# Three hand-overs of an encoder: weight operands in idle token tiles, Newton steps behind the sums, rates one product later

## Chip, core and metric

The kernel runs on one core of one Trainium2 chip. The metric is the device time of one execution in microseconds (us): the median of three runs. The core's engines have queues of their own: PE (TensorE, matrix products), DVE (VectorE, elementwise), ACT (ScalarE, elementwise), SP (which issues the DMAs).

## What is computed

An encoder of two residual layers over one sequence of 512 tokens with 1024 channels, in float32. Layer 0 mixes tokens by a Fourier transform, layer 1 by retention with four heads; each is followed by a SwiGLU channel mixer. Every sub-layer begins with an RMS norm, whose result is scaled and shifted by vectors that come from a conditioning vector c; one norm stands at the end.

```
for i in range(DEPTH):                       # DEPTH = 2
    mod = c_act @ w_ada[i] + b_ada[i]
    sh1, sc1, g1, sh2, sc2, g2 = jnp.split(mod, 6, axis=-1)
    h = modulate(rmsnorm(x, norm_mix_g[i]), sh1, sc1)
    m = fourier_mixer(h, w_o) if i % 2 == 0 else retention_mixer(h, w_in, w_out, ...)
    x = x + g1 * m
    h = modulate(rmsnorm(x, norm_ffn_g[i]), sh2, sc2)
    x = x + g2 * swiglu(h, w_ffn_in[i], w_ffn_out[i])
return modulate(rmsnorm(x, final_norm_g), shf, scf)
```

## The kernel before

**Operands.** x is held transposed, channels on the 128 partitions, in four tiles `x0` to `x3`. A float32 product is made of three passes with rounded operands: every operand is split into a high part (a cast on ACT, L201 in `split`) and a low part (source minus high, on DVE, L202), and PE adds high by high, high by low and low by high. Weights arrive by DMA in `raw` tiles of 128x1024 (eight buffers, loaded up to four ahead by `issue`), and `high_low` splits each into a tile of the pool `high` and one of the pool `low`, five buffers each.

**Units.** The wide products (kinds "v", "qk", "g" of retention, "fi" of the channel mixer) are done by `Unit`, 512 tokens by 512 columns at a time, with seven quarter-size products in place of eight. Each product has a tag ("1", "2", "7", "6", "5", "3", "4") and is 24 matmuls of 128x256 on PE (L874). Its weight operand is a quarter or a sum of quarters; the sums are made on DVE by `combined` (L333). Its token operand is one of seven that `Quarters` makes from the modulated x, each a high and a low tile that is held for the whole stage (`a0` to `a6` the highs, `a7` to `a13` the lows). Tags "1" and "2" need only the first 256 tokens (t = 0), the other five also need the last 256 (t = 1). A finished quarter of the result is taken out of PSUM by an ACT copy (L883) and a DVE addition (L887).

**A turn.** A stage ends in `out_product_last`: the output product of the half of tokens t = 0 and then of t = 1, each piece added to x on DVE (L546, `add_gated`). Behind the additions the norm of the next stage runs: `sums` transposes squares-to-be on PE (L418), squares and sums them on ACT (L424), and scales the sums on DVE (L426, L428); `rate` runs three Newton steps on two columns on DVE (`rsqrt_steps`, L218, L226, L229) and turns the two columns into a row on PE (two transposes, L439); `half` modulates x (L462 on DVE, L466 and L467 on ACT) and makes the token operands (L493, L512, L202). For t = 0 this is done inside the output product. For t = 1 it is done by `first_units`, while the first products of the next stage (tags "1" and "2" of the first three units u0, u1, u2) run on PE. There are three such turns: into the channel mixer of layer 0 (`channels=True`, about 100 to 152 us of the trace; called A here), into retention (465 to 547 us; B) and into the channel mixer of layer 1 (893 to 938 us; C). The last turn, into the final norm, has no Units behind it.

**What sets the order.** The order of work comes from the list `program` that `first_units` and its like fill, from the step list that makes weight operands ahead of their use (`use_next`), and from a scheduler that places each instruction in its engine's queue; the norm's work stands under `tc.high_priority`. An engine takes its queue strictly in order. In turn B the retention's queries and keys are rotated by DVE operations at L1015 to L1018 before the first scores (L207 to L209 with `t4k` operands).

Of the kernel before, what the change touches and what calls it, by code (L numbers as in the profile page):

```python
# [11 lines left out]
F32R = mybir.dt.float32r  # L12
# [4 lines left out]
P = 128  # L17
D = 1024
# [18 lines left out]
URGENT = 500  # L37
# [116 lines left out]
def trunk(ctx, tc, A, where, out):  # L154
# [7 lines left out]
    highs = pool("high", 5)  # L162
    lows = pool("low", 5)
# [7 lines left out]
    def ps():  # L171
        return psum.tile([P, 512], F32, name="ps")
# [7 lines left out]
    def held(tag, dtype=F32R):  # L180

        return hpool.tile([P, D], dtype, name=tag)

    def tok(m):
        return slice(m * P, (m + 1) * P)
# [10 lines left out]
    def k4(t):  # L196
        return t.rearrange("p (k c) -> p k c", k=4)

    def split(dst_h, dst_l, src):

        nc.scalar.copy(out=dst_h, in_=src)  # L201
        nc.vector.tensor_tensor(out=dst_l, in0=src, in1=f32(dst_h), op=ALU.subtract)  # L202
# [33 lines left out]
    def rsqrt_of(columns):  # L236
        ys = []
        for _ in rsqrt_steps(columns, ys):
            pass
        return ys  # L240
# [31 lines left out]
    def add(fn, *needs):  # L272
        program.append((needs, fn))

    steps, at, fresh = [], {}, []
    state = {"step": 0, "load": 0, "piece": 0}
    loads, ready, mods, opening, wide = {}, {}, {}, set(), set()
    closing, shares = [], {(0, 1): 2, (0, 0): 2, (0, 3): 4, (0, 4): 4}

    def pieces_of(step):  # L280
# [23 lines left out]
            loads[name] = t  # L304
            state["load"] += 1

    def high_low(raw):
        h = highs.tile([P, D], F32R, name="high")
        low = lows.tile([P, D], F32R, name="low")
        split(h, low, raw)  # L310
        return h, low

# [13 lines left out]
    def combined(step):  # L326


        kind, i, u, tag, _ = step
        r = lambda k, s: loads[kind, i, u, k, s]  # L330

        def minus(dst, p, q, eng=nc.vector):
            eng.tensor_tensor(out=dst, in0=p, in1=q, op=ALU.subtract)  # L333

        if tag == "1":
            o = high_low(r(0, 0))
        elif tag == "2":
            o = high_low(r(1, 0))
            if (kind, i, u) not in opening:
                minus(r(0, 0), r(0, 1), r(0, 0))  # L340
        elif tag == "7":
            if (kind, i, u) in opening:
                minus(r(0, 0), r(0, 1), r(0, 0))
                minus(r(0, 1), r(1, 1), r(0, 1))
            o = high_low(loads.pop((kind, i, u, 0, 1)))
        elif tag == "6":
            t2 = comb.tile([P, D], F32, name="t2")
            minus(t2, r(1, 1), r(0, 0))
            minus(r(1, 0), r(1, 0), t2)
            o = high_low(t2)  # L350
            if (kind, i, u) not in opening:
                minus(r(0, 1), r(1, 1), r(0, 1))
        else:
            o = high_low(loads.pop((kind, i, u, *{"5": (0, 0), "3": (1, 1), "4": (1, 0)}[tag])))
        return k4(o[0]), k4(o[1])
# [48 lines left out]
    class Norm:  # L404


        def __init__(self, i, sc, sh):
            self.key = (i, sc), (i, sh)
            self.turned, self.mean, self.r = {}, {}, {}
            self.start()  # L410

        def sums(self, t, j):

            for c in range(2):
# [15 lines left out]
                        )  # L430
                self.mean[t, c] = ss

        def rate(self, t):
            o = ps()
            self.r[t] = o[:, 0:256]
            with tc.high_priority(offset=URGENT):
                rs = rsqrt_of([self.mean[t, c] for c in range(2)])
            for c, r in enumerate(rs):
                nc.tensor.transpose(o[:, tok(c)], r.broadcast_to([P, P]), ident)  # L439

        def spread(self, t, k):
            for key in self.key:
                settle(key, 4 * k + 3)
            with tc.high_priority(offset=URGENT):
                for _ in self.half(t, k):
                    pass
# [162 lines left out]
    def last_sums():  # L609
        for j in range(ND - SUMS, ND):  # L610
            made["norm"].sums(1, j)

    made = {}

# [278 lines left out]
    def first_units(u0, u1, u2, channels=False):  # L893


        for u in (u0, u1, u2):
            opening.add(u.key)
        wide.add(u1.key)
        spread = lambda t, k: add(lambda: made["norm"].spread(t, k))
        if channels:  # L900
            add(last_sums)
            u0.p("1")
            u1.p("1")
            add(lambda: made["norm"].rate(1))
            spread(1, 0)
            u2.p("1")
            spread(0, 1)
            u0.ps("72")
            spread(1, 1)
            u1.p("2")  # L910
            u2.p("2")
        else:
            u0.p("1")
            add(last_sums)
            u0.p("2")
            u1.p("1")
            add(lambda: made["norm"].scale(1))
            u1.p("2")
            u2.ps("12")
            u0.p("7")  # L920
        for u, t in ((u0, "6"), (u1, "7"), (u0, "5"), (u1, "6"), (u0, "3"), (u0, "4"), (u1, "5")):
            u.p(t)
# [353 lines left out]
```

## Time and profile before

| | us |
|---|---|
| runs | 1263.14, 1263.08, 1271.62 |
| median | 1263.14 |
| profiled execution | 1267.04 |
| its span, first to last instruction | 1265.3 |
| PE busy | 1207.9 (95%) |
| DVE busy | 1066.0 (84%) |
| ACT busy | 585.2 (46%) |

A row of a timeline gives start, duration, engine, line, operation, output and inputs, how many were merged, and in brackets how long the engine stood idle ahead of it and for whom. Durations overlap: the distance between the starts of neighbours is what one costs. A row of waits gives who waited at which line for whose result, the total, the number and the longest, in us. A row of windows gives, for a stretch, the busy time of each engine with the number of instructions, the granted TensorE clock as a share of 2.4 GHz, the DMA's share and its rate.

### The profile page before, as it was taken

The numbers are of one execution on the slowest core, as the hardware profiler recorded it, in microseconds if no ns is written. First come the engines' busy times: TensorE is split into PE (matmuls) and PEld (weight loads), VectorE is DVE, ScalarE is ACT, GpSimd is POOL, SyncE is SP. The second block draws the span as 40 slices with busy tenths as digits, with TensorE's granted clock in tenths as the row PEclk, the third lists the DMA queues.
The fourth block names the chain that finished last, engine by engine and source line by source line (L and its number), as shares of the span: only waits on it lengthen the run. The fifth ranks groups of instructions, "written<-read, shape, count | busy, mean of one in ns | idle before, by whom it ended". The sixth has DMA issues, their size and how long they took to land.

```text
span 1265.3 us, 20931 instructions
## 1 busy us (share of the span) xinstructions
PE 1207.9 (95%) x8424; PEld 1134.1 (90%) x8424; DVE 1066.0 (84%) x1733; ACT 585.2 (46%) x885; POOL 0.9 (0%) x8
## 2 busy tenths in 40 slices
PE   6898799999999998889999999999899999999996
PEld 5787799899999998879999999988899899999986
DVE  7799999889799779989899899964899777878855
ACT  4615654343435436536365454521665334444523
POOL 0000000000000000000000000000000000000000
PEclk9999899999999999899999999999999999999999
DMA  9486068464644621314233245872024434344402
GB/s 369 171 297 243 17 186 286 138 223 135 217 133 154 213 101 66 103 64 141 91 101 115 84 151 183 309 238 100 18 70 155 158 115 155 117 150 133 134 1 67
DMA packets 59440, 186.64 MB, mean 148 GB/s; under 512 B 5968, under 2 KB 14544, under 8 KB 59344
## 3 DMA queue, kind: packets, MB, share of 16 engines
q1 hardware_dynamic: 59344, 185.31, 43.3%
q8 instruction: 66, 1.08, 0.4%
q14 instruction: 30, 0.25, 0.1%
HBM read 177.95 MB, written 7.34 MB: 146 GB/s over the span
## 4 chain that ended last, share of the span: by engine, by line
PE 85%; DVE 8%; ACT 4%; issue 1%; DMA 1%; SPq 0%; ACTq 0%
PE ps L874 48%; PE ps L207 12%; PE ps L209 11%; PE ps L208 11%; DVE low L202 2%; DVE a L202 1%; ACT t4k L467 1%; ACT high L201 1%; PE ps L418 1%; DVE t4k L493 1%; ACT a L466 1%; DVE raw L383 1%; DVE raw L333 1%; DMA t4k<-in_x 1%; PE ps L1094 1%
## 5 line engine op out<-in xcount | busy, mean ns | idle before, releaser
L201 ACT CAST high<-raw 128x1024 fp32r<-128x1024 f32 x266 | 277.7, 1051 | 298.7 <-PE ps L208 96.9
L874 PE MATMUL ps<-a,high 128*128 128x256 f32 x2912 | 392.2, 285 | 3.7 <-ACT a L512 2.8
L202 DVE TENSOR_TENSOR low<-raw,high 128x1024 fp32r<-128x1024 f32 x266 | 323.6, 1221 | 63.6 <-ACT high L201 61.5
L874 PEld LDWEIGHTS ps<-a,high 128*128 128x128 f32 x2912 | 370.9, 193 | 6.1 <-ACT a L512 3.0
L874 PE MATMUL ps<-a,low 128*128 128x256 f32 x1456 | 208.7, 287 | 8.0 <-DVE low L202 7.9
L874 PEld LDWEIGHTS ps<-a,low 128*128 128x128 f32 x1456 | 191.1, 195 | 8.9 <-DVE low L202 8.9
L207 PE MATMUL ps<-t4k,high 128*128 128x512 f32 (+1 forms) x512 | 182.2, 356 | 0.0
L208 PE MATMUL ps<-t4k,high 128*128 128x512 f32 (+1 forms) x512 | 179.0, 350 | 0.0
L209 PE MATMUL ps<-t4k,low 128*128 128x512 f32 (+1 forms) x512 | 178.7, 349 | 0.0
L383 DVE SCALAR_TENSOR_TENSOR raw<-raw,c_act 128x1024 f32<-128x1024 f32 x104 | 125.9, 1221 | 34.1 <-DMA raw<-in_w_ada 23.3
L874 PE MATMUL ps<-high,a 128*128 128x256 f32 x896 | 122.8, 284 | 4.6 <-ACT t2k L883 3.7
L874 PEld LDWEIGHTS ps<-high,a 128*128 128x128 f32 x896 | 114.8, 192 | 6.3 <-ACT t2k L883 4.1
L209 PEld LDWEIGHTS ps<-t4k,low 128*128 128x128 f32 x512 | 96.6, 189 | 12.7
L207 PEld LDWEIGHTS ps<-t4k,high 128*128 128x128 f32 x512 | 96.7, 189 | 11.9
L208 PEld LDWEIGHTS ps<-t4k,high 128*128 128x128 f32 x512 | 96.9, 189 | 11.6
L546 DVE SCALAR_TENSOR_TENSOR x<-ps,mod,x 128x512 f32<-128x512 f32 (+1 forms) x132 | 81.0, 634 | 29.7 <-PE ps L209 29.5
L883 ACT COPY t2k<-ps 128x512 f32<-128x512 f32 x102 | 59.6, 585 | 99.9 <-PE ps L874 96.8
L887 DVE TENSOR_TENSOR t2k<-t2k,ps 128x512 f32<-128x512 f32 x102 | 69.6, 683 | 12.4 <-ACT t2k L883 7.1
L333 DVE TENSOR_TENSOR raw<-raw 128x1024 f32<-128x1024 f32 x62 | 75.5, 1218 | 0.1
L874 PE MATMUL ps<-low,a 128*128 128x256 f32 x448 | 63.7, 285 | 0.0
L201 ACT CAST t4k<-t2k 128x512 fp32r<-128x512 f32 x76 | 46.8, 619 | 35.6 <-DVE t2k L939 20.0
L874 PEld LDWEIGHTS ps<-low,a 128*128 128x128 f32 x448 | 58.6, 194 | 0.0
(142 smaller groups left out, 1325.5 us busy)
## 6 DMA issues: line engine op xcount, KB each, us to landing
raw<-in_w_ada SPq DMA_DIRECT2D x88, 512.0 KB, 4.7
raw<-in_w_ffn_in SPq DMA_DIRECT2D x84, 512.0 KB, 4.2
raw<-in_w_ret_in SPq DMA_DIRECT2D x46, 512.0 KB, 3.3
raw<-in_w_ffn_out SPq DMA_DIRECT2D x44, 512.0 KB, 4.0
raw<-in_w_ret_out SPq DMA_DIRECT2D x16, 512.0 KB, 4.4
raw<-in_w_ada_final SPq DMA_DIRECT2D x16, 512.0 KB, 3.7
raw<-in_w_fourier_out SPq DMA_DIRECT2D x8, 512.0 KB, 6.9
z<-t2k SPq DMA_DIRECT2D x12, 256.0 KB, 3.1
```

Of the source, the lines that this page charges most:

```text
L201: nc.scalar.copy(out=dst_h, in_=src)
L202: nc.vector.tensor_tensor(out=dst_l, in0=src, in1=f32(dst_h), op=ALU.subtract)
L207: nc.tensor.matmul(o, ah, bh, start=first, stop=False, **kw)
L208: nc.tensor.matmul(o, ah, bl, start=False, stop=False, **kw)
L209: nc.tensor.matmul(o, al, bh, start=False, stop=last, **kw)
L333: eng.tensor_tensor(out=dst, in0=p, in1=q, op=ALU.subtract)
L383: nc.vector.scalar_tensor_tensor(out=t, in0=t, scalar=1.0, in1=c_act, op0=ALU.mult, op1=ALU.mult, accum_out=v[:, q : q + 1])
L418: nc.tensor.transpose(o[:, tok(j % 4)], xt(j)[:, part(t)][:, tok(c)], ident)
L546: nc.vector.scalar_tensor_tensor(out=xt(j)[:, sl], in0=o, scalar=mods[key][:, j : j + 1], in1=xt(j)[:, sl], op0=ALU.mult, op1=ALU.add)
L874: nc.tensor.matmul(o[:, j * 256 : (j + 1) * 256], a, b, start=tag in "127" and n == m == j == k == 0, stop=n == 1 and k == 3, skip_group_c ...
L883: nc.scalar.copy(out=t, in_=o)
L887: nc.vector.tensor_tensor(out=t, in0=t, in1=self.z if tag == "5" else o, op=ALU.add)
```

## The change

Three edits, in `high_low`/`combined`, in `Norm` and in `first_units`. The arithmetic and the number of operations are the same.

1. For turns B and C, four weight operands (u0 "1", u0 "2", u1 "1", u2 "1") are split into held token tiles (pairs a4/a11, a2/a9, a5/a12, a3/a10), not into the pools `high` and `low`. 
2. The Newton steps become a method of their own, `steps`, called at the end of `last_sums`; `rate` then only has the two transposes (for t = 0 it still calls `steps` itself).
3. u2's product "1" stands ahead of the rates and the modulation of t = 1: ahead of `rate(1)` in A, ahead of `scale(1)` in B and C.

```
-    def high_low(raw):
-        h = highs.tile([P, D], F32R, name="high")
-        low = lows.tile([P, D], F32R, name="low")
+    def high_low(raw, step=None):
+        if step in homes:
+            h, low = (held(f"a{n}") for n in homes[step])
+        else:
+            h = highs.tile([P, D], F32R, name="high")
+            low = lows.tile([P, D], F32R, name="low")
         split(h, low, raw)
         return h, low
...
         if tag == "1":
-            o = high_low(r(0, 0))
+            o = high_low(r(0, 0), step)
         elif tag == "2":
-            o = high_low(r(1, 0))
+            o = high_low(r(1, 0), step)
...
+        def steps(self, t):
+            with tc.high_priority(offset=URGENT):
+                self.rs[t] = rsqrt_of([self.mean[t, c] for c in range(2)])
+
         def rate(self, t):
+            if t not in self.rs:
+                self.steps(t)
             o = ps()
             self.r[t] = o[:, 0:256]
-            with tc.high_priority(offset=URGENT):
-                rs = rsqrt_of([self.mean[t, c] for c in range(2)])
-            for c, r in enumerate(rs):
+            for c, r in enumerate(self.rs[t]):
                 nc.tensor.transpose(o[:, tok(c)], r.broadcast_to([P, P]), ident)
...
             made["norm"].sums(1, j)
+        made["norm"].steps(1)
...
         wide.add(u1.key)
+        if not channels:
+            order = [(u0, "1"), (u0, "2"), (u1, "1"), (u2, "1")]
+            homes.update({(*u.key, t, 0): h for (u, t), h in zip(order, [(4, 11), (2, 9), (5, 12), (3, 10)])})
...
             u0.p("1")
             u1.p("1")
+            u2.p("1")
             add(lambda: made["norm"].rate(1))
             spread(1, 0)
-            u2.p("1")
             spread(0, 1)
...
             u0.p("2")
             u1.p("1")
+            u2.p("1")
             add(lambda: made["norm"].scale(1))
             u1.p("2")
-            u2.ps("12")
+            u2.p("2")
             u0.p("7")
```

**Turn B on PE**, from the product u1 "1" on (`a_4803` and `a_4804` are the high and the low of the first token operand, `a_4820` and `a_4821` of the second, `rs_y` the Newton columns). Before:

```order
L874 MATMUL ps<-a_4803,high 128x256 x8
L874 MATMUL ps<-a_4803,low 128x256 x8
L874 MATMUL ps<-a_4804,high 128x256 x8
L439 MATMUL ps<-ident,rs_y_5035 128x128
L874 MATMUL ps<-a_4820,high 128x256 x8
L874 MATMUL ps<-a_4820,low 128x256
L439 MATMUL ps<-ident,rs_y_5036 128x128
L874 MATMUL ps<-a_4820,low 128x256 x7
L874 MATMUL ps<-a_4821,high 128x256 x8
```

With the change (`a_4619`/`a_4620` and `a_4625`/`a_4626` are weight operands in held tiles):

```order
L882 MATMUL ps<-a_4803,a_4619 128x256 x8
L882 MATMUL ps<-a_4803,a_4620 128x256 x8
L882 MATMUL ps<-a_4804,a_4619 128x256 x8
L882 MATMUL ps<-a_4625,a_4803 128x256 x8
L882 MATMUL ps<-a_4626,a_4803 128x256 x8
L882 MATMUL ps<-a_4625,a_4804 128x256 x8
L446 MATMUL ps<-ident,rs_y_4961 128x128
L446 MATMUL ps<-ident,rs_y_4962 128x128
L882 MATMUL ps<-a_4820,high 128x256 x8
```

The product u2 "1" stands ahead of the two transposes, which now stand together; before, the transposes stood ahead of and inside the next product.

**Turn B on DVE**, behind the last additions to x, with buffer numbers. Before, up to the first Newton operation and the weight low that follows:

```order
L333 TENSOR_TENSOR raw_4469<-raw_4469,t2_5103 128x1024
L202 TENSOR_TENSOR low_4626<-raw_4509,high_4625 128x1024
L428 SCALAR_TENSOR_TENSOR ss06_4944<-ss06_4944,ss03_4867 128x1
L202 TENSOR_TENSOR low_4913<-raw_4543,high_4912 128x1024
L428 SCALAR_TENSOR_TENSOR ss16_4948<-ss16_4948,ss13_4871 128x1
L428 SCALAR_TENSOR_TENSOR ss07_4953<-ss07_4953,ss06_4944 128x1
L333 TENSOR_TENSOR raw_4503<-t4k_4910,raw_4503 128x1024
L428 SCALAR_TENSOR_TENSOR ss17_4958<-ss17_4958,ss16_4948 128x1
L887 TENSOR_TENSOR t2k_4941<-t2k_4941,ps_4967 128x512
L218 TENSOR_SCALAR rs_y0_5035<-ss07_4953 128x1
L218 TENSOR_SCALAR rs_y1_5036<-ss17_4958 128x1
L202 TENSOR_TENSOR low_4964<-raw_4549,high_4963 128x1024
```

With the change:

```order
L336 TENSOR_TENSOR raw_4503<-t4k_4910,raw_4503 128x1024
L431 SCALAR_TENSOR_TENSOR ss06_4944<-ss06_4944,ss03_4867 128x1
L431 SCALAR_TENSOR_TENSOR ss16_4948<-ss16_4948,ss13_4871 128x1
L202 TENSOR_TENSOR low_5056<-t2_5052,high_5055 128x1024
L431 SCALAR_TENSOR_TENSOR ss07_4953<-ss07_4953,ss06_4944 128x1
L431 SCALAR_TENSOR_TENSOR ss17_4958<-ss17_4958,ss16_4948 128x1
L336 TENSOR_TENSOR t4k_4910<-t4k_4979,t4k_4910 128x1024
L218 TENSOR_SCALAR rs_y0_4961<-ss07_4953 128x1
L218 TENSOR_SCALAR rs_y1_4962<-ss17_4958 128x1
L895 TENSOR_TENSOR t2k_4941<-t2k_4941,ps_4985 128x512
L226 SCALAR_TENSOR_TENSOR rs_u0_4963<-rs_y0_4961,ss07_4953 128x1
L226 SCALAR_TENSOR_TENSOR rs_u1_4964<-rs_y1_4962,ss17_4958 128x1
```

Three 1024-wide lows of weights (`low_4626`, `low_4913`, `low_4964`) no longer stand in this stretch; they have gone ahead of the last additions to x. Turn C shows the same pattern.

**Turn A on DVE**, around the low of u2's weight "2" (`low_1362`); `a9`, `a10`, `a12` and `a13` are lows of token operands. Before:

```order
L493 TENSOR_TENSOR t4k_1068<-t4k_1409,t4k_1068 128x512
L887 TENSOR_TENSOR t2k_1207<-t2k_1207,ps_1382 128x512
L493 TENSOR_TENSOR t4k_1068<-t4k_1409,t4k_1068 128x512
L493 TENSOR_TENSOR t4k_1260<-t4k_1260,t4k_1409 128x1024
L202 TENSOR_TENSOR a9_1419<-t4k_1068,a2_1418 128x512 x2
L202 TENSOR_TENSOR a12_1428<-t4k_1260,a5_1427 128x1024
L493 TENSOR_TENSOR t4k_1311<-t4k_1311,t4k_1068 128x1024
L202 TENSOR_TENSOR a13_1437<-t4k_1409,a6_1436 128x1024
L887 TENSOR_TENSOR t2k_1237<-t2k_1237,ps_1444 128x512
L202 TENSOR_TENSOR a10_1433<-t4k_1311,a3_1432 128x1024
L202 TENSOR_TENSOR low_1362<-raw_1179,high_1361 128x1024
L333 TENSOR_TENSOR t2_1365<-raw_1151,raw_1137 128x1024
```

With the change:

```order
L500 TENSOR_TENSOR t4k_1068<-t4k_1409,t4k_1068 128x512
L202 TENSOR_TENSOR low_1362<-raw_1197,high_1361 128x1024
L500 TENSOR_TENSOR t4k_1068<-t4k_1409,t4k_1068 128x512
L202 TENSOR_TENSOR a9_1419<-t4k_1068,a2_1418 128x512
L500 TENSOR_TENSOR t4k_1293<-t4k_1293,t4k_1409 128x1024
L895 TENSOR_TENSOR t2k_1225<-t2k_1225,ps_1382 128x512
L202 TENSOR_TENSOR a9_1419<-t4k_1068,a2_1418 128x512
L202 TENSOR_TENSOR a12_1428<-t4k_1293,a5_1427 128x1024
L500 TENSOR_TENSOR t4k_1311<-t4k_1311,t4k_1068 128x1024
L202 TENSOR_TENSOR a13_1437<-t4k_1409,a6_1436 128x1024
L895 TENSOR_TENSOR t2k_1255<-t2k_1255,ps_1444 128x512
L202 TENSOR_TENSOR a10_1433<-t4k_1311,a3_1432 128x1024
```

`low_1362` stood behind the token lows and now stands in front of them; the sum of weights `t2_1365` still follows the last token low.

## Rows read from the trace of the kernel before

**Rows 1.** The page's busy time of engines, share of the span, instructions.

```profile
PE 1207.9 (95%) x8424; PEld 1134.1 (90%) x8424; DVE 1066.0 (84%) x1733; ACT 585.2 (46%) x885; POOL 0.9 (0%) x8
```

**Rows 2.** Windows; columns: stretch, length, PE, PEld, DVE, ACT, POOL, clock, DMA, GB/s.

```profile
425.00:468.00 43.00, 43.00 (x294) 39.91 (x292) 27.29 (x54) 12.04 (x23) 0.00 (x0) 1.00 0.28 98
468.00:547.00 79.00, 68.58 (x522) 66.51 (x520) 74.93 (x120) 47.93 (x81) 0.00 (x0) 0.94 0.29 100
843.00:893.00 50.00, 50.00 (x299) 44.67 (x298) 25.25 (x51) 9.94 (x19) 0.00 (x0) 1.00 0.32 106
116.00:128.00 12.00, 5.76 (x47) 5.33 (x46) 11.83 (x33) 8.21 (x14) 0.00 (x0) 1.00 0.53 176
138.00:152.00 14.00, 7.76 (x48) 7.38 (x48) 14.00 (x15) 5.50 (x7) 0.00 (x0) 0.76 0.00 1
488.00:491.40 3.40, 3.40 (x18) 3.40 (x18) 3.34 (x7) 0.51 (x1) 0.00 (x0) 0.53 0.47 154
509.70:516.20 6.50, 6.46 (x32) 6.46 (x33) 5.46 (x6) 1.67 (x2) 0.00 (x0) 0.55 0.23 83
915.00:925.00 10.00, 10.00 (x73) 10.00 (x73) 8.13 (x16) 6.77 (x13) 0.00 (x0) 0.83 0.00 0
938.00:960.00 22.00, 22.00 (x185) 22.00 (x185) 21.67 (x24) 11.95 (x16) 0.00 (x0) 1.00 0.46 150
```

**Rows 3.** Timeline of PE, turn B.

```profile
473.59 0.44 PE L418 MATMUL ps<-ident,x 128*128 128x128 f32 x2 [0.69 <-DVE x L546]
...
481.68 1.12 PE L874 MATMUL ps<-a,high 128*128 128x256 f32 x8
482.64 1.12 PE L874 MATMUL ps<-a,low 128*128 128x256 f32 x8
483.60 1.12 PE L874 MATMUL ps<-a,high 128*128 128x256 f32 x8
487.85 0.32 PE L439 MATMUL ps<-ident,rs_y 128*128 128x128 f32 x1 [3.13 <-DVE rs_y L229]
...
546.21 0.73 PE L207 MATMUL ps<-t4k 128*128 128x512 f32 x2 [0.64 <-ACT t4k L201]
```

**Rows 4.** Timeline of DVE, turn B.

```profile
488.85 0.15 DVE L229 SCALAR_TENSOR_TENSOR rs_y<-rs_u,rs_y 128x1 f32<-128x1 f32 x1
488.92 1.22 DVE L333 TENSOR_TENSOR t4k<-t4k 128x1024 f32<-128x1024 f32 x1
490.20 2.44 DVE L462 SCALAR_TENSOR_TENSOR t4k<-x,mod,ps 128x256 f32<-128x256 f32 x6
494.24 1.49 DVE L493 TENSOR_TENSOR t4k<-t4k 128x512 f32<-128x512 f32 x2 [1.60 <-ACT t4k L467]
...
517.03 0.69 DVE L887 TENSOR_TENSOR t2k<-t2k,ps 128x512 f32<-128x512 f32 x1 [1.86 <-ACT t2k L883]
...
546.55 0.69 DVE L202 TENSOR_TENSOR t4k<-t2k,t4k 128x512 fp32r<-128x512 f32 x1
```

**Rows 5.** Waits of PE, turn C, 890 to 940 us.

```profile
PE ps L439 <- DVE rs_y L229: 3.7, 1, 3.7
PE ps L418 <- DVE x L546: 0.7, 1, 0.7
```

**Rows 6.** Timeline of DVE, turn C: last Newton step, modulation.

```profile
914.83 0.16 DVE L229 SCALAR_TENSOR_TENSOR rs_y<-rs_u,rs_y 128x1 f32<-128x1 f32 x1
914.90 1.22 DVE L333 TENSOR_TENSOR t<-t4k,raw 128x1024 f32<-128x1024 f32 x1
916.03 2.44 DVE L462 SCALAR_TENSOR_TENSOR t4k<-x,mod,ps 128x256 f32<-128x256 f32 x6
```

**Rows 7.** Timeline of PE, turn A.

```profile
121.42 0.32 PE L439 MATMUL ps<-ident,rs_y 128*128 128x128 f32 x1 [3.46 <-DVE rs_y L229]
...
127.53 1.33 PE L874 MATMUL ps<-a,high 128*128 128x256 f32 x9 [2.78 <-ACT a L512]
...
143.55 2.07 PE L874 MATMUL ps<-a,low 128*128 128x256 f32 x8 [6.17 <-DVE low L202]
```

**Rows 8.** Waits of DVE, 425 to 468 us.

```profile
DVE low L202 <- ACT high L201: 6.5, 4, 3.6
```

More of the change, by code (lines that the diff above doesn't have):

```diff
@@ L276, in trunk @@
     state = {"step": 0, "load": 0, "piece": 0}
-    loads, ready, mods, opening, wide = {}, {}, {}, set(), set()
+    loads, ready, mods, opening, wide, homes = {}, {}, {}, set(), set(), {}
     closing, shares = [], {(0, 1): 2, (0, 0): 2, (0, 3): 4, (0, 4): 4}
@@ L408, in __init__ @@
             self.key = (i, sc), (i, sh)
-            self.turned, self.mean, self.r = {}, {}, {}
+            self.turned, self.mean, self.r, self.rs = {}, {}, {}, {}
             self.start()
```

## Prediction

> **What bounds the kernel now.** I read the page's busy times first, then the windows, the waits of PE, and the timelines of PE and DVE around the turns. PE is busy for 1207.9 of 1265.3 us, 95% [rows 1], so a change that leaves the matmuls alone can only win back PE's idle time and the time in which its granted clock is at the lower of its two levels (1.2 against 2.4 GHz). Both gather in the turns. In the stretches ahead of B and C, 425 to 468 and 843 to 893, PE is busy all the time at full clock, while DVE does 27.29 of 43 and 25.25 of 50 us [rows 2]: there DVE has room, 15.7 and 24.8 us. In turn B, 468 to 547, PE is busy 68.58 of 79 us and DVE 74.93 [rows 2]: there DVE is full, and PE idles 10.4 us. On top of this come two slow stretches: 3.4 us at 0.53 and 6.5 us at 0.55 [rows 2], worth 3.4 x 0.47 = 1.6 and 6.5 x 0.45 = 2.9 us. So B loses 14.9 us. In C, PE waits 3.7 us for the Newton result and 0.7 for the last addition to x [rows 5], and the ten microseconds from 915 have a clock of 0.83 [rows 2], worth 1.7: 6.1 us. In A, PE waits 3.46, 2.78 and 6.17 us [rows 7].
>
> **Part 1, the home tiles.** No operation is added. In the pools, operands for the first products queue behind the five buffers that the running output product holds; in the held tiles they can be made before the last additions to x. By the orders, five 1024-wide DVE operations leave the stretch between those additions and the scores in B: nine stand from the last addition but one to the modulation before and seven now, and behind the modulation, up to the scores, there are three fewer. One costs 1.13 us, start to start (914.90 to 916.03 [rows 6]), so 5 x 1.13 = 5.7 us leave a full DVE for a stretch in which it has 15.7 us free (24.8 in C). The casts that belong to them lie on ACT, which does 12.04 of 43 and 9.94 of 50 us there [rows 2]. I cost them at nothing ahead of the turn. If that cover were gone, the five would cost their 5.7 us again, and the move would only shift the wait.
>
> The home tiles must be empty when they are filled and read out when the tokens come. The token operand of tag "6" overwrites u0 "2"'s weight first; PE reads that weight in its second product of the turn, over before 481.68, where the third begins, and DVE does not reach the modulation of t = 1 before 487. That wait is nothing.
>
> **Parts 2 and 3, Newton steps and rates.** In B, PE stands 3.13 us ahead of the transposes at 487.85 [rows 3], since the last Newton step of the first column ends just then, and that of the second at 489.0 [rows 4]; behind them it runs slowly. With the change one more product lies ahead of the transposes, three passes 0.96 us apart, 2.88 us [rows 3], and the Newton steps lose two operations ahead of them, 2.3 us; PE itself comes 0.69 us earlier, since the last additions do (the wait at 473.59 [rows 3]). Its wait becomes 3.13 − 2.88 − 2.3 + 0.69, below zero by 1.4. The two transposes now stand together, so the second column counts, 1.1 us after the first: still no wait. The 3.13 and 0.69 us and the 1.6 us of slow clock behind are gone on PE, and the modulation starts at 490.20 − 2.3 = 487.9 [rows 4]. The DVE steps themselves only change places: 14 short operations, the same as before.
>
> But PE's gain counts only as far as DVE lets it keep it. The scores need the low of the rotated keys, whose last piece DVE starts at 546.55 [rows 4], and DVE is the full engine up to there. Its chain shortens by the 2.3 us ahead of the modulation, by 3 x 1.13 = 3.4 behind it, and by the two idle times 1.60 and 1.86 us [rows 4], which are waits for ACT. I take these as gone, since the first halves are now combined between modulations (ACT gets a start), and the copy at 517.03 follows a PE that is no longer late. That gives 2.3 + 3.4 + 3.5 = 9.2 us, key lows at 537.4. PE's own work would allow the first scores at 546.2 − 14.9 = 531.3, so PE will stand up to 6 us ahead of the scores.
>
> **What that wait costs.** After 3.13 us idle the clock was 0.53 for 3.4 us; after idle times of 3.46 and 2.78 us in A it stayed at 1.00 [rows 2, 3, 7]. I take the first, 1.6 us; the bounds are 0 and the 2.9 of the longer slow stretch. The Trainium skill, "TensorE: Matmul & The Clock Gate", Part 1 (The HAM clock gate), says that the throttled clock is the default and that only activity releases it; the row at 0.53 agrees with it, the 1.00 of turn A does not for waits of that size. By the rule alone the longer wait would be followed by the full slow stretch, 1.3 us more than I take.
>
> So **B gains 9.2 − 1.6 = 7.6 us**. Lower bound: the two DVE waits for ACT stay and the slow stretch is the long one, 5.7 − 2.9 = 2.8. Upper: 9.2.
>
> **Turn C.** The same order, but there are no scores: behind the turn PE is busy 22.00 of 22 us with DVE at 21.67 [rows 2], so what PE gains it keeps if DVE gains as much. The modulation moves from 916.03 [rows 6] by 2.3 to 913.7, and DVE has 3.4 less behind it: 5.7 in all. On PE the 0.7 us go, and the wait for the Newton steps becomes 3.7 − 2.88 − 2.3 + 0.7, below zero by 0.8; the second column, 1.2 us after the first, leaves a wait of 0.4. The 1.7 of slow clock go with it. **C gains 6.1 − 0.4 = 5.7 us**, the same from either engine. Bounds: 2.3, if only the modulation's advance is kept, and 6.1.
>
> **Turn A.** No home tiles here. The Newton steps have the same DVE work ahead, so the transposes stay. u2's product "1" fills 2.88 of the 3.46 us [rows 7], and `low_1362`, for which PE stood 6.17 us, moves ahead of the token lows. But in 138 to 152 DVE is busy 14.00 of 14 us [rows 2]: the sums of weights behind the last token low come when they came, and PE, earlier by up to 6 us, waits for them instead. **A gains 0**, between −1.6 (one more short slow stretch) and +0.5 (DVE's small gaps).
>
> **Sum.** 7.6 + 5.7 + 0 = 13.3 us. The profiled execution of 1267.0 would become 1253.7; it lies 3.9 above the median, and nothing ties this difference to the turns, so I take the gain from the median: 1263.1 − 13.3 = **1249.8 us**. The bounds give 2.8 + 2.3 − 1.6 = 3.5 (1259.6) to 9.2 + 6.1 + 0.5 = 15.8 (1247.3).
>
> **The rivals.**
>
> *DVE's waits for ACT stay in B.* The key lows then come 5.7 us earlier and not 9.2; with the same 1.6 of clock B gains 4.1, in all 9.8: 1253.3. For it: ACT's modulation has to follow DVE's whatever the order. Against: by the order, work stands between the two.
>
> *The stalls are only moved.* The home tiles are not filled early, because their weights' loads or casts still wait, so DVE's five operations stay in the turn. For it: DVE waits 6.5 us in four places for casts in 425 to 468 already [rows 8]. Then B and C keep the lower bounds, 1263.1 − 3.5 = 1259.6.
>
> *Slower: the home weights starve the output product.* Their raw tiles and their place in the in-order queues lie ahead of weights that the output product needs. If each of some five such weights came late by 3.6 us, the longest wait for a cast [rows 8], PE would lose 5 x 3.6 = 18 us in a stretch where it idles for none, and the time would be 1249.8 + 18 = 1268. It decides from 13.3 us of new idle time in 425 to 468 and 843 to 893 on. Against: PE's clean 43.00 and 50.00 us [rows 2] with that 3.6 already in them say that the weights are well ahead.
>
> *More is gained*: the scores' wait stays at full clock and C's is zero, or later stretches profit from a DVE that is ahead: 1246.
>
> **How the numbers follow.** Chances: forecast (1247.3 to 1253) 0.53; waits for ACT stay 0.24; only moved 0.13; starved 0.04; more 0.06. The range 1246 to 1258 leaves out the starved case and most of the moved one, some 2 in 10 with the far side of the last. About 1% (12.6 us) is what a measurement of this kernel tells from no change; that bound lies at 1250.5, so the forecast stands just beyond it: 0.34 of its 0.53 and the 0.06 of the last case give faster 0.40; slower 0.02, if two turns starve, which costs 36; the rest, 0.58, is within 1%.
>
> **What would show it.** Right: PE without a wait at the transposes in B and under 1 us in C; the modulation some 2.3 us sooner after the last addition to x; a PE wait of 4 to 6 us ahead of the first scores in B and none of 2 us before; full clock behind the transposes in B and C; no new PE idle time ahead of the turns; in A the 6.17 us broken into smaller waits with the same end. Wrong: waits of DVE for ACT casts inside the turns as long as before, PE idle in 425 to 468 or 843 to 893, or a turn A that ends later than 152 us against its stage's start.

## The result, and the profile after

| | before | after |
|---|---|---|
| runs beside each other, us | 1263.08 to 1271.71 (4), median 1267.38 | 1246.87 to 1254.84 (4), median 1250.87 |
| ratio, 95% interval | | 0.9877, 0.9831 to 0.9924 |
| timed again (11 and 6 runs), us | 1258.86 to 1271.67, median 1261.94 | 1246.16 to 1254.98, median 1246.64 |
| ratio, 95% interval | | 0.9884, 0.9844 to 0.9925 |

By the two ratios the change is worth 14.6 to 15.6 us, 1.2%, and both intervals lie clear of no change; 13.3 were forecast. Executions of either kernel fall into two groups some 8 us apart, which differ in the first 35 us and not by the change (last section); before's spread more widely within a group, and its turn A varies (below). So the time of one execution says less than a stretch of its trace. I therefore measure the turns inside the traces, between the starts of the same matmuls of PE, counted from the first: A from number 480 to 960, B from 2640 to 3720, C from 5760 to 6300. Each holds the whole turn and nothing of the start. (First 480: from the first matmul to number 480.)

| trace | first 480 | A | B | C |
|---|---|---|---|---|
| before | 103.2 | 74.88 | 165.49 | 71.60 |
| before, profiled again | 94.8 | 78.85 | 164.24 | 71.34 |
| after | 95.3 | 76.46 | 157.83 | 65.22 |
| after, profiled again | 94.9 | 76.26 | 157.90 | 65.20 |

B gained 7.7 us (6.3 against the second profile of before), C 6.4 (6.1), and A lies between the two profiles of before. Outside the turns and the start nothing moved: in all 14 traces of this document the stretch between A and B takes 237.6 to 237.8 us, that between B and C 298.5 to 298.7, and what follows C 311.2 to 311.4. The busy times of the page of after; PE's fell from 1207.9, but more than half of that belongs to the start of this execution (PE was busy 1202.1 us in the second profile of before and 1199.1 in that of after):

```profile
PE 1197.2 (96%) x8424; PEld 1125.5 (90%) x8424; DVE 1064.3 (85%) x1733; ACT 585.1 (47%) x885; POOL 0.9 (0%) x8
```

Windows of after (stretch, length, PE, PEld, DVE, ACT, POOL, clock, DMA, GB/s): the stretches ahead of B and C, then B and C:

```profile
419.00:462.00 43.00, 43.00 (x294) 39.94 (x293) 32.55 (x59) 16.18 (x27) 0.00 (x0) 1.00 0.28 98
829.00:879.00 50.00, 50.00 (x298) 44.62 (x297) 28.94 (x53) 13.62 (x23) 0.00 (x0) 1.00 0.29 98
462.00:533.00 71.00, 63.47 (x512) 61.99 (x511) 69.94 (x116) 43.79 (x77) 0.00 (x0) 0.97 0.34 111
886.00:925.00 39.00, 38.72 (x324) 38.42 (x323) 38.48 (x67) 27.30 (x51) 0.00 (x0) 1.00 0.19 65
```

These are the stretches of [rows 2], 6 and 14 us earlier. DVE now does 32.55 of 43 us ahead of B where it did 27.29, and PE still runs without a gap: the home tiles' work is there, under PE's cover. In turn C, PE has lost 0.28 us in 39.

Waits of PE in after, first turn B (455 to 545 us), then turn C (870 to 930), which answer [rows 3] and [rows 5]:

```profile
PE ps L882 <- ACT t2k L891: 4.3, 3, 2.4
PE ps L207 <- ACT t4k L201: 2.7, 1, 2.7
PE ps L882 <- DVE low L202: 0.5, 1, 0.5
...
PE ps L446 <- DVE rs_y L229: 0.3, 1, 0.3
```

The waits of 3.13 and 3.7 us at the transposes have become none and 0.3. The timelines of DVE in B and C answer [rows 4] and [rows 6] (last Newton step, modulation, and in B the last low of the keys):

```profile
480.57 0.15 DVE L229 SCALAR_TENSOR_TENSOR rs_y<-rs_u,rs_y 128x1 f32<-128x1 f32 x1
480.63 1.22 DVE L336 TENSOR_TENSOR raw<-raw,t 128x1024 f32<-128x1024 f32 x1
481.77 1.65 DVE L469 SCALAR_TENSOR_TENSOR t4k<-x,mod,ps 128x256 f32<-128x256 f32 x4
...
531.59 0.69 DVE L202 TENSOR_TENSOR t4k<-t2k,t4k 128x512 fp32r<-128x512 f32 x1
...
898.92 0.15 DVE L229 SCALAR_TENSOR_TENSOR rs_y<-rs_u,rs_y 128x1 f32<-128x1 f32 x1
...
900.12 1.65 DVE L469 SCALAR_TENSOR_TENSOR t4k<-x,mod,ps 128x256 f32<-128x256 f32 x4
```

At the start of B after is 6.15 us ahead of before, and at the start of C 13.78. On before's axis the Newton steps of B so end at 486.9 (2.1 us earlier; 2.3 forecast), the modulation starts at 487.9 (487.9) and the last key low at 537.7 (537.4); in C the Newton steps end at 912.9, also 2.1 earlier, and the modulation starts at 913.9 (913.7).

### The profile page after: what moved, and what is told of

It reads as the page before. It is cut to its first block, busy times and chain, and to the rows that moved or that the text cites. A ratio compares the mean times of both kernels' runs of the same rounds, so it can differ in the third digit from the quotient of the medians.

```text
span 1245.1 us, 20911 instructions
## 1 busy us (share of the span) xinstructions
PE 1197.2 (96%) x8424; PEld 1125.5 (90%) x8424; DVE 1064.3 (85%) x1733; ACT 585.1 (47%) x885; POOL 0.9 (0%) x8
## 4 chain that ended last, share of the span: by engine, by line
PE 88%; DVE 6%; ACT 4%; DMA 1%; issue 1%; SPq 0%; ACTq 0%
PE ps L882 51%; PE ps L207 12%; PE ps L208 12%; PE ps L209 12%; DVE low L202 1%; ACT t4k L474 1%; PE ps L421 1%; ACT a L473 1%; DVE raw L386 1%; DVE a L202 1%; DMA t4k<-in_x 1%; ACT high L201 1%; PE ps L1106 1%; DVE raw L336 0%; PE ps L792 0%
## 5 line engine op out<-in xcount | busy, mean ns | idle before, releaser
L201 ACT CAST high<-raw 128x1024 fp32r<-128x1024 f32 x258 | 269.7, 1051 | 279.7 <-PE ps L208 90.0
L882 PE MATMUL ps<-a,high 128*128 128x256 f32 x2832 | 381.1, 285 | 10.2 <-ACT a L519 5.9
L882 PEld LDWEIGHTS ps<-a,high 128*128 128x128 f32 x2832 | 360.6, 193 | 12.7 <-ACT a L519 6.1
L202 DVE TENSOR_TENSOR low<-raw,high 128x1024 fp32r<-128x1024 f32 x258 | 313.9, 1221 | 54.2 <-ACT high L201 52.9
L882 PE MATMUL ps<-a,low 128*128 128x256 f32 x1416 | 200.5, 285 | 1.0 <-DVE low L202 1.0
L882 PEld LDWEIGHTS ps<-a,low 128*128 128x128 f32 x1416 | 184.2, 194 | 1.3 <-DVE low L202 1.3
L882 PE MATMUL ps<-high,a 128*128 128x256 f32 x848 | 115.6, 283 | 3.6 <-ACT t2k L891 3.6
L882 PEld LDWEIGHTS ps<-high,a 128*128 128x128 f32 x848 | 108.4, 192 | 4.9 <-ACT t2k L891 4.0
L882 PE MATMUL ps<-low,a 128*128 128x256 f32 x424 | 60.2, 284 | 0.5 <-DVE low L202 0.5
L202 DVE TENSOR_TENSOR t4k<-t2k,t4k 128x512 fp32r<-128x512 f32 x76 | 52.0, 686 | 7.1 <-ACT t4k L201 7.1
```

What stands on the lines that cost most here:

```text
L882: nc.tensor.matmul(o[:, j * 256 : (j + 1) * 256], a, b, start=tag in "127" and n == m == j == k == 0, stop=n == 1 and k == 3, skip_group_c ...
```

## The experiments

The turns, in us, of each kernel that was run, with the waits of PE that matter. The rows of before and after above belong beside them.

| kernel | A | B | C |
|---|---|---|---|
| third edit alone | 76.17 | 163.95 | 70.13 |
| second and third | 76.25 | 163.79 | 70.09 |
| first alone, three tiles | 77.70 | 157.62 | 70.25 |
| all, A as before | 74.85 | 159.32 | 65.21 |
| all without the second | 76.49 | 156.03 | 65.55 |
| all without the second, again | 76.37 | 156.05 | 65.55 |
| all, three home tiles | 76.36 | 156.81 | 67.47 |
| all, PE kept running | 77.01 | 156.68 | 65.21 |
| all, DVE +2 early | 76.38 | 157.05 | 67.30 |
| all, DVE +2 late | 76.33 | 157.10 | 68.91 |

**The third edit alone.**

```
             u1.p("1")
+            u2.p("1")
             add(lambda: made["norm"].rate(1))
             spread(1, 0)
-            u2.p("1")
...
             u1.p("1")
+            u2.p("1")
             add(lambda: made["norm"].scale(1))
             u1.p("2")
-            u2.ps("12")
+            u2.p("2")
```

> The kernel before with the third edit alone: u2's product 1 ahead of the rates in all three turns, no home tiles, Newton steps where they were. I read the turns as the time between the same matmuls of PE (A from the 480th to the 960th, B from the 2640th to the 3720th, C from the 5760th to the 6300th), which were 74.9, 165.5 and 71.6 us before and 76.5, 157.8 and 65.2 with the whole change. My theory (DVE is the full engine in B and C, and only the home tiles take work out of it): the wait at the transposes shrinks by up to 2.9 us but comes back as waits for DVE further on; B 164 to 166, C 69 to 71.5, A 76.5. Rival (PE's order is what counts, the tiles are a detail): B 158 to 161, C 65 to 67.

Measured: B 163.95, C 70.13. The waits of PE in C (890 to 940 us):

```profile
PE ps L874 <- DVE low L202: 2.2, 2, 1.2
PE ps L439 <- DVE rs_y L229: 0.9, 1, 0.9
PE ps L418 <- DVE x L546: 0.7, 1, 0.7
```

The wait at the transposes fell from 3.7 to 0.9, but 2.2 us came back as waits for weight lows, which are still made inside the turn. That is the theory's picture; the rival falls. In B more happened than its 1.5 us show. The last key low came 3.5 us earlier (124.63 us into B, before 128.13), since DVE's two waits for ACT are gone with this edit too; but PE ran at half clock from 540.7 to 550.9 us, and from the first scores to the end of B it took 39.7 us, where before took 37.7.

**The change without the first edit.**

```
-        if not channels:
+        if False:
             order = [(u0, "1"), (u0, "2"), (u1, "1"), (u2, "1")]
```

> The whole change without its first edit: Newton steps behind the sums and u2's product 1 ahead of the rates, all weight operands in the pools. My theory: no DVE work leaves the turns, so B 163 to 166 and C 68.5 to 71, A 76.5. Rival (order of PE and of the Newton steps is enough): B 158 to 160, C 65 to 67.

B 163.79, C 70.09: within 0.2 us of the third edit alone in both turns, so without the tiles the moved Newton steps do nothing.

**The first edit alone, with three tiles.** To the kernel before are added the new `high_low`, its two calls with `step`, and

```
+        if not channels:
+            order = [(u0, "1"), (u0, "2"), (u1, "1")]
+            homes.update({(*u.key, t, 0): h for (u, t), h in zip(order, [(4, 11), (2, 9), (5, 12), (3, 10)])})
```

> The kernel before with the first edit alone, with three home tiles, not four (u0 1, u0 2, u1 1), since the fourth is only free for a weight if u2's product 1 stands ahead of the token operand that takes its tile. My theory: four of the five DVE operations leave B, and the waits of DVE for ACT behind them shrink, so B 158 to 161; in C the modulation comes 2.3 us earlier and PE's wait at the transposes becomes 3.7 - 2.3 + 0.7 = 2.1, so C 67 to 69.5; A 74.9, as before. Rival: B 164 to 166 and C 70.5 to 72, because PE still stands in front of the transposes.

B 157.62, as short as with the whole change; C 70.25, a smaller gain than expected. Waits of PE in C (870 to 940 us):

```profile
PE ps L442 <- DVE rs_y L229: 3.3, 1, 3.3
PE ps L877 <- DVE low L202: 0.2, 1, 0.2
```

Here the picture is turned around: the waits for x and for lows are gone, and the one at the transposes stays at 3.3, not the 2.1 I had worked out. In C the two edits take away different waits, and each alone leaves one that eats most of the gain: 1.4 us for the first with three tiles, 1.5 for the third. All edits with three tiles gain 4.1 (below), with four 6.4. In B, PE still stood 2.7 us at the transposes. That the turn was as short as with the whole change does not make this wait free: after has a stretch at half clock at the scores that this kernel has not. Like with like, three tiles and no slow stretch in B, the kernel with all edits takes 156.81 (below), 0.8 less.

**The change with turn A as before.**

```
-            u2.p("1")
             add(lambda: made["norm"].rate(1))
             spread(1, 0)
+            u2.p("1")
             spread(0, 1)
```

> The whole change, but in turn A u2's product 1 stays between the two halves of the modulation, as before. In the changed kernel PE waits 5.9 us in one piece in A for a token operand and then runs 10.2 us at the lower clock, where the kernel before had 3.5 and 2.8 us with the product between them, and full clock. My theory: the wait in one piece is what brings the slow stretch, so A goes back to 74.9 (from 76.5), B and C stay at 157.8 and 65.2. Rival (A is bound by DVE, whose order with the Newton steps moved is what cost the 1.6 us): A stays at 76.0 to 76.5.

A was 74.85, as the theory had it; but the kernel with the first edit alone has before's order in A as well, and there A was 77.70. So this run settles nothing about A by itself, and I profiled the kernel before once more.

**The kernel before, again.**

> The kernel before, profiled once more, to see what one execution differs from the next. In the traces so far the first 480 matmuls took 103 to 104 us in four kernels and 95 in two, at the same order of instructions, and turn A, with the same instructions and the same waits, took 74.9 us in two kernels and 77.7 in one, where two more slow stretches of the clock stand in it. My theory: this is the clock and differs between executions of one kernel; the first 480 matmuls take 95 or 103 to 104, A 74.9 or up to 77.7, B 165.5 within 2, C 71.6 within 2, with the same waits of PE within 0.1 us. Rival: it belongs to the kernels, and this profile repeats the first one within 0.2 us everywhere.

A was 78.85, 4.0 us longer than in the first profile. The waits of PE in A (95 to 157 us) are the same as there:

```profile
PE ps L874 <- DVE low L202: 6.2, 1, 6.2
PE ps L439 <- DVE rs_y L229: 3.5, 1, 3.5
PE ps L874 <- ACT a L512: 2.8, 1, 2.8
```

The windows of this profile show what differs: two stretches of A at half clock that the first profile does not have (its clock is 1.00 from the start of A to 140 us):

```profile
112.30:119.10 6.80, 5.81 (x26) 5.52 (x26) 5.22 (x15) 2.74 (x4) 0.00 (x0) 0.50 0.71 234
122.60:126.00 3.40, 3.40 (x18) 3.40 (x17) 3.40 (x8) 3.37 (x8) 0.00 (x0) 0.50 0.00 0
```

Theory right, and a little beyond its bound (77.7). Over the traces, A with before's order took 74.85, 74.88, 77.70 and 78.85; with the changed order it took 76.17 to 76.49 in nine, always with a stretch of 10.2 us at half clock that sets in during a wait of 5.5 to 5.9 us. The mean is 76.6 against 76.3: in A the change does nothing that these runs can show, except that its time varies less. What A follows is DVE. Windows of exactly A, in the first and then the second profile of before (DVE's busy time is the fifth column, as in [rows 2]):

```profile
105.92:180.80 74.88, 60.79 (x482) 59.22 (x481) 73.85 (x124) 46.72 (x76) 0.00 (x0) 0.95 0.36 117
```

```profile
97.60:176.45 78.85, 64.78 (x482) 63.28 (x481) 73.94 (x124) 46.78 (x76) 0.00 (x0) 0.89 0.34 112
```

DVE is busy 73.8 to 74.0 us of A in all 14 traces, and A is longer by what DVE idles: 1.0 us in the first profile, 4.9 in the second, where one of its operations waited 2.2 us for ACT and one 1.9 for PE. So the clock counts in A as far as it makes DVE wait.

**PE kept running.**

```
+        def fill(self, t, n):
+            h = self.h["1"]
+            o = ps()
+            for _ in range(n):
+                nc.tensor.matmul(o[:, 0:256], h[:, 0, 0:P], h[:, 0, 0:256], start=True, stop=True)
...
             add(lambda: made["norm"].rate(1))
+            add(lambda: made["norm"].fill(1, 40))
...
+            if "filled" not in r:
+                r["filled"] = True
+                h = made["norm"].op("1")[0]
+                for _ in range(20):
+                    nc.tensor.matmul(sc[:, 0:256], h[:, 0, 0:P], h[:, 0, 0:256], start=True, stop=True)
```

> The changed kernel with matmuls added whose results are overwritten or never read: 40 of 128x256 (4.8 us at full clock) behind the rates of turn A, where PE waits 5.9 us, and 20 (2.4 us) ahead of the first scores in B, where it waits 2.7 us. They add work to PE and nothing to the other engines. My theory: the lower clock behind PE's waits is what cost turn A its 1.6 us and part of B's gain; with PE kept running the slow stretch of 10.2 us in A goes and A falls from 76.5 to 74.9 or a little below, and B from 157.8 to 156 to 157. Rival: DVE is the bound in both places and the clock costs nothing; A stays at 76 to 76.5 and B at 157.8 or becomes longer by the added work.

In B the theory held. Windows from 526 to 535 us, first of after, then of this kernel: the clock is 0.64 and 1.00.

```profile
526.00:535.00 9.00, 5.34 (x21) 4.49 (x22) 8.54 (x11) 1.54 (x3) 0.00 (x0) 0.64 0.22 71
```

```profile
526.00:535.00 9.00, 7.46 (x47) 6.24 (x45) 9.00 (x13) 1.76 (x4) 0.00 (x0) 1.00 0.21 64
```

The first scores began 119.0 us into B in both, and from there to the end of B it took 38.9 us in after and 37.7 here (37.7 too in before): the lower clock behind the waits ahead of the scores costs 1.2 us. Where B met a second slow stretch earlier on, in the kernel with A as before, it took 159.3. In A the theory failed. The stretch at 0.50 (115.5 to 125.7) shrank to 3.4 us, yet A took 77.0. DVE's work there is the same 73.9 us, and the scheduler had moved a DVE addition that reads PSUM ahead of two operations that could have run, so that DVE stood for PE:

```profile
127.93 0.69 DVE L901 TENSOR_TENSOR t2k<-t2k,ps 128x512 f32<-128x512 f32 x1 [2.03 <-PE ps L888]
```

In after that addition waited 0.32 us. So the experiment changed two things in A, and how long A would be with the clock alone changed is not shown; below DVE's 73.9 us it could not go.

**The change without the second edit.**

```
             made["norm"].sums(1, j)
-        made["norm"].steps(1)
+        pass
```

> The changed kernel without its second edit: the Newton steps of the last half of the tokens are issued in the rate again, behind u2's product 1. My theory: the second edit alone does next to nothing, since the scheduler places the steps early by their priority either way; B 157.6 to 159.3, C 65.2 to 65.8, and PE's wait at the transposes stays under 1 us. Rival: the moved steps are what took the wait away; PE waits 1 to 3 us at the transposes in C again and C becomes 66.5 to 69.

C 65.55, wait at the transposes 0.4 us: the second edit is worth 0.3 us in C, and the rival falls. B was shorter, 156.03, which neither side expected: DVE's order there differs in a few places, the last key low comes 0.6 us earlier than in after, the largest wait of PE is 2.2 us, and no slow stretch stands in B. Beside the changed kernel, timed on one chip:

> The changed kernel without its second edit, timed beside it. My theory (the second edit does nothing that can be measured, and the scheduler's other small moves in B avoid a slow stretch ahead of the scores): 0 to 2 us less than the changed kernel, B 156 to 158, C 65.5, A 76.5. Rival (its gain in the first profile was the clock's luck): equal within 0.5 us, B 157.5 to 159.

> The changed kernel as it is, timed against the kernel before on one chip. From the traces, the turns sum to about 12 us less than before, give or take the clock's 4 us in A and 1 to 2 in B, and the first 480 matmuls take 95 or 103 us in either kernel. My theory: ratio 0.9877 to 0.991 (11 to 15.5 us), with both starts seen in both kernels. Rival (the early start belongs to the change): the ratio is 0.984 or less, and the changed kernel never takes the late start.

The ratios to before are 0.9896 (0.9857 to 0.9934) without the second edit and 0.9884 (0.9844 to 0.9925) with it: no difference that these times can tell. The early and the late start occur in both (1244.58 to 1246.08 and 1253.29 to 1255.13; 1246.16 to 1246.97 and 1254.45 to 1254.98), which rules out that the early one belongs to the change. B was 156.05 again, against 157.83 and 157.90 in the two profiles of after: the second edit costs 1.8 us in B, 1.2 of them by the slow stretch at the scores.

**Three home tiles.**

```
-            order = [(u0, "1"), (u0, "2"), (u1, "1"), (u2, "1")]
+            order = [(u0, "1"), (u0, "2"), (u1, "1")]
```

> The changed kernel with three home tiles: u2's product 1 keeps its place ahead of the rates, but its weight operand is made in the pools. My theory: each 1024-wide DVE operation that stays in a turn costs at most its 1.13 us: C 65.2 to 66.4 with a wait of up to 1.4 us at the transposes, B 156 to 159.4. Rival: the fourth tile is what lets the three edits work together; without it C goes back to 69 to 70, where either edit alone left it.

B 156.81, no loss; C 67.47, between the two expectations. Its waits (870 to 930 us):

```profile
PE ps L882 <- DVE low L202: 1.7, 2, 1.2
PE ps L446 <- DVE rs_y L229: 0.3, 1, 0.3
```

One operation of 1.13 us put back into C made two waits, each for the low of a weight, 1.7 us in all, and 2.25 us of time: more than its own length.

**Two DVE operations more, early and late.** The first placed them under high priority in `scale`, reading x; the second in `half`, reading the sum that is just made (`turn` is set to 0 in A and to 1 in B and C, in a line not shown):

```
+            for _ in range(2 if isinstance(self, Quarters) else 0):
+                with tc.high_priority(offset=URGENT):
+                    nc.vector.tensor_tensor(out=held("a13"), in0=x[0], in1=x[0], op=ALU.subtract)
```

```
                 combine(a12, a12, a11, ALU.subtract)
+                if made["turn"] > 0:
+                    for _ in range(2):
+                        combine(held("a13"), a12, a12, ALU.subtract)
                 parts("3", a12)
```

> The changed kernel with two more 1024-wide DVE operations in each of the turns B and C, behind the last additions to x, whose result (a tile that is overwritten later) is not used: 2 x 1.13 = 2.3 us. My theory (DVE sets the end of B, and in C its Newton steps set PE's wait): B grows by 2.3 plus or minus the clock's share, to 158.5 to 161.5; C by 2.3 to 4 (wait at the transposes 2.5 instead of 0.28, with the lower clock behind it), to 67.5 to 69.2. Rival (PE sets the pace, DVE has room again after the change): B and C grow by less than 1 us.

> The changed kernel with two more 1024-wide DVE operations in each of the turns B and C, this time behind the modulation and ahead of the token low of tag 3 (they read a token sum that is only just made, so that they cannot be placed earlier; what they write is overwritten later): 2 x 1.13 = 2.3 us. The two operations of the run before had been placed ahead of the last additions to x, so they only told what 2 us of waiting of PE cost there: 2.1 us in C, nothing in B. My theory (B ends with the DVE chain up to the scores, C with PE): B grows by 2.3, from 156.0 to 157.9 (with the clock's share) to 158.3 to 160.2, with PE waiting that much more ahead of the scores; C grows by less, 0 to 1.5, since DVE has caught up there (no wait of PE behind the transposes). Rival (both turns end with PE and B's waits come from ACT): B within 1 us of 156.0 to 157.9, C 65.2 to 65.5.

The early ones landed ahead of the rates of t = 0, a product stage earlier than meant: PE waited 2.0 us there in both turns, and 0.3 for x. C grew by 2.1, about those waits. B took 157.05, less than after's 157.83, but without the slow stretch at the scores, which is worth 1.2; like with like it grew by 0.4. The late ones landed where they should. I expected B to grow by their 2.3 us and C by less. It was the other way: B was 157.10, C 68.91, 3.7 more, with this wait of PE (870 to 930 us) and behind it 3.4 us at half clock (917.3 to 920.7), worth 1.7:

```profile
PE ps L885 <- DVE low L202: 1.9, 1, 1.9
```

So in the changed kernel C has no slack on DVE left. For B the result says less than its number does. Windows from the last addition to x to the last key low, of before, after, the first edit alone and the two late operations:

```profile
477.64:546.55 68.91, 59.23 (x448) 57.76 (x446) 65.00 (x100) 39.18 (x60) 0.00 (x0) 0.93 0.24 84
468.81:531.59 62.78, 55.33 (x452) 54.31 (x451) 61.77 (x101) 37.87 (x64) 0.00 (x0) 0.98 0.30 100
477.46:541.21 63.75, 56.55 (x464) 55.52 (x463) 62.89 (x102) 38.80 (x65) 0.00 (x0) 1.00 0.31 99
468.21:531.84 63.63, 57.45 (x461) 56.64 (x460) 62.80 (x101) 37.95 (x64) 0.00 (x0) 0.97 0.29 99
```

The scheduler had put a weight sum of the same width behind the keys, so DVE got only one operation more ahead of them: 62.80 us busy against 61.77, and the last key low came 0.9 us later (120.2 us into B, 119.3 in after). With the first edit alone it is one operation too, 62.89 us, and 1.0 later (120.28). So DVE's work ahead of the keys does count about one for one. B still did not grow because PE had no slow stretch at the scores this time: from there to the end it took 37.0 us, in after 38.9.

## Why the prediction came out right, step by step

**The first edit moves DVE work under PE's cover: right.** DVE ahead of B went from 27.29 to 32.55 us of 43, PE stayed at 43.00, and the modulations came 2.3 and 2.1 us earlier, as worked out from net two operations. Neither turn starves the output product (PE has no wait in 419 to 462 or 829 to 879), and the operations did leave the turns, so the slower rival and that of the stalls only moved both fall.

**B is set by the DVE chain to the key lows: right, with a part of the clock in it.** In every trace the last key low starts 0.1 to 0.4 us behind the first matmul of the scores, whose next pass needs it, and from that matmul to the end of B it is 37.0 to 39.7 us. Key lows come 8.8 us earlier (128.1 to 119.3 us into B) against 9.2 forecast. The last addition to x comes 2.7 us earlier, and from there on DVE has 3.2 us less work and 2.9 us less idle time (the windows above; 5.7 were forecast for the first two together, 3.5 for the idle time). DVE's waits for ACT, 1.6 and 1.9 before, are gone:

```profile
DVE ss L431 <- ACT ps L427: 0.3, 1, 0.3
DVE t2k L895 <- PE ps L882: 0.2, 1, 0.2
DVE a L500 <- ACT a L519: 0.2, 1, 0.2
```

(waits of DVE in after, 464 to 532 us). The clock behind the wait ahead of the scores cost 1.2, where I took 1.6. Both slips cancel: 7.6 forecast, 7.7 found. The size of the clock's term was luck: I took a stretch of 3.4 us, and one of 6.8 came (528.6 to 535.4). It cost so little because 2.6 us of it passed while PE stood anyway, and because PE's waits of 0.4 and 1.4 us behind the first scores, which before has, are gone in after. What I missed is that the chain is not DVE's alone. In the second profile of before, with the same work on DVE, the wait of 1.86 is 0.59 and the last key low starts 126.85 us into B, not 128.13: the second slow stretch of PE in B is 3.4 us long there and 6.8 in the first. Against that profile B gained 6.3, not 7.7.

**The wait ahead of the scores: right in sum.** "Up to 6 us" came as waits of 2.45 and 2.69 us, ending 4.2 us apart.

**C: right in kind, 0.7 too small.** 5.7 forecast, 6.4 found (6.1 against the second profile). The transposes' wait is 0.28 where I kept 0.4, and the small wait for a low behind the turn (0.36 before) had been left out of the 6.1; the last 0.2 stay open. That DVE gains no more than PE, as forecast, means that DVE has no slack: adding 2.3 us of its work cost 3.7.

**The second edit: mis-described.** I said that the Newton steps end earlier because two DVE operations ahead of them are gone, and that is what is measured; the edit itself is worth 0.3 us in C and costs 1.8 in B. The prediction has no term for it.

**A: the forecast of 0 holds, and so does its reason, but A is not a constant.** The sum of weights behind the last token low does come when it came (38.1 us into A, before 37.5), and DVE's 73.9 us of work are the same in every trace and fill A. With unchanged waits of PE it takes 74.9 or 78.9, by DVE's idle time. The first profile of before showed almost the shortest A, and I had taken that for the usual one. This is also why the measured gain (14.6 to 15.6) exceeds the sum of the turns in the first two traces (12.5): between the second profile of before and the second of after the three turns differ by 2.6 + 6.3 + 6.1 = 15.1. With both profiles of each kernel the turns differ by 13.8 in the mean, next to the 13.3 forecast.

**The time itself: luck.** 1249.8 us were forecast and the median is 1250.87, but no run lies near either: the four took 1246.87, 1247.44, 1254.30 and 1254.84, two in each group, and the median falls between. The base was a like matter. I set aside the 3.9 us by which the profiled execution of before lay above the median because nothing tied them to the turns. Against the second profile, 5.8 us shorter in all, its start was 8.4 us longer, its A 4.0 shorter, and B and C 1.5 longer together.

## What to carry to other kernels

Where two edits remove two waits of one stretch, test them apart and together: in C either edit alone, with three tiles or none, gave 1.4 to 1.5 us and both with three tiles 4.1, because the engine only moved on to the next wait. An operand that is known early should be made in a tile that is idle early, not in the pool of the stage that is still running; what it is worth is read in the stretch that it leaves, if the one that takes it has room. Before a stall's price is taken from one profile, look whether the same waits give the same time in a second one. When an experiment adds work to an engine, count what stands in the stretch afterwards: the scheduler may have moved other work out.

## What was not expected of the hardware

The first 480 matmuls, the same instructions in all kernels, took 94.5 to 95.3 us in eight traces and 102.9 to 104.6 in six. The difference is TensorE's clock, as the distance between the starts of like matmuls tells. In the first profile of before PE is busy without a gap from 20 to 30 us, and its matmuls of 128x256 start 0.21 us apart until 34.2; in the second they start 0.12 apart from 16.9 on. PE in the first and then the second profile of before:

```profile
33.35 0.41 PE L209 MATMUL ps<-a,a 128*128 128x256 f32 x1
33.57 0.42 PE L207 MATMUL ps<-a,a 128*128 128x258 f32 x1
...
34.36 0.28 PE L208 MATMUL ps<-a,a 128*128 128x256 f32 x1
34.48 0.28 PE L209 MATMUL ps<-a,a 128*128 128x256 f32 x1
```

```profile
15.60 0.41 PE L208 MATMUL ps<-a,a 128*128 128x256 f32 x1
15.81 0.41 PE L209 MATMUL ps<-a,a 128*128 128x256 f32 x1
...
17.08 0.28 PE L207 MATMUL ps<-a,a 128*128 128x256 f32 x1
17.19 0.28 PE L208 MATMUL ps<-a,a 128*128 128x256 f32 x1
```

So a busy PE can stay at 1.2 GHz for over ten microseconds at the start of one execution and not of the next; what decides it, no run here shows. The profile's clock column has 1.00 in this stretch; its first record is a rise to 1.00 at 34.26 us in the first profile and at 16.77 in the second, where the distance of the starts changes. Half of the 17.5 us between is 8.7, next to the 8.4 by which the first 480 matmuls differ. The Trainium skill, "TensorE: Matmul & The Clock Gate", Part 1 (The HAM clock gate), holds that a busy engine releases the throttle; the late start does not fit that alone.
